# Second FFN of a hybrid diffusion step: first weights loaded before the output stage, the input's remaining blocks in a set order, inner rows stored whole and split in the down stage

## The chip, the cores and the metric

The kernel runs on one core of a Trainium2 chip. The metric is device time in microseconds (us) of one execution. Before the change three runs gave 3045.46, 3050.65 and 3051.04 us, median 3050.65. Engines: PE (TensorE matmuls; PEld is its weight load), DVE (VectorE), ACT (ScalarE), POOL (GpSimd), SP (SyncE, which here only issues DMAs).

## The reference

The reference is two layers of a backbone, 1024 latent and 128 context tokens, model width 1024. Each layer is a mixer and a gated conv FFN with sandwich norms. The change touches the FFN of the second layer:

```python
def conv_ffn(h, w_up, cw, cb, w_down):
    u = dwconv(h @ w_up, cw, 1) + cb          # w_up 1024 x 5632, 3 taps over tokens
    g, val = jnp.split(u, 2, axis=-1)
    return (jax.nn.gelu(g) * val) @ w_down    # w_down 2816 x 1024
xs = _post(xs, conv_ffn(_pre(xs, m_s, norm_g[l, 2], 1), *ffw), m_s, norm_g[l, 3], 1)
```

All of it is float32.

## The kernel before

T = 1152 tokens stand in NT = 9 tiles of 128; the FFN's inner 2816 channels in NFB = 22 blocks of 128. A float32 matmul is made of three fast ones: each operand is split into a high part (a copy into the type F32R on ACT) and a low part (a subtraction on DVE or POOL), and hi·hi, hi·lo and lo·hi are added up in PSUM (`pair`, L1519, and `split` functions).

**The output stage before the FFN** (`mixer_out`, L1390): for each token tile, a 1024x1024 product, the norm and residual, the next norm, a transpose, and `Blocks.put`, which writes the FFN's input.

**The FFN's input as blocks** (`Blocks`, L57). The up product uses a scheme with 7 products in place of 8: the input is cut into quarters 11, 12, 21, 22 (channels by tokens, half each) and weights likewise; each block of 128 channels and its gate partner needs the products of `PRODS` (L1560): S2·T2, S1·T1, w11·11, S4·22, w12·21, S3·T3, w22·T4. S1 to S4 are sums of weight quarters, T1 to T4 of input quarters. `put` makes T1 and T2 and splits them as the tiles come. `rest` (L91) splits 11, 22, 21 and builds and splits T3 and T4: for each of six items four chunks of 128x576.

**The up stage** (`up`, L1526): for block n `load` brings the weights of value and gate (512 KB each) on SP's queue; `split(n, i)` makes the weight sums on POOL and the split of product i, on POOL for i = 0 and 3, on DVE otherwise; `prod` runs 24 matmuls of 128x288; `evict` adds the products together; `up_rest` (L1642) is the convolution (rows of three taps, ACT once, DVE four times), the gelu, the product with the value (L1665), the split of that row (copy L1666 on ACT, subtraction L1667 on POOL) and two stores to DRAM (L1669). `order` runs the products of block n with product 6 of block n-1 behind the first of block n. Weights are loaded two blocks ahead, and weight splits have three buffers. `H.rest` stands in the program behind the first product.

**The down stage** (`early` in `layers`, L1970, and `down2`, L1690): three groups of 8, 7 and 7 blocks; for each group and token tile, `down_rows` (L1682) loads hi and lo rows of that tile from DRAM with two DMAs on POOL's queue (three buffers), 48 or 42 matmuls of 128x512 follow, and the sums are copied (first group, ACT) or added (DVE, L1714). `down_w` (L1674) loads one block of w_down on SP's queue and splits it on DVE or POOL. `early` starts the first of both before the up stage's last product is out.

**What sets the order.** The program that builds the kernel orders each engine's instructions itself, from estimated durations: it issues what its estimate has ready, earlier in the program first. Waits are placed by it for every dependence. A new pool of buffers lies over the memory of closed ones, and its buffers wait for what was there. `behind(i, p)` (L183) forces i after p on one engine.

Of the kernel before, what the change touches and what calls it, by code (L numbers as in the profile page):

```python
# [17 lines left out]
T = 1152  # L18
# [38 lines left out]
class Blocks:  # L57
# [12 lines left out]
    def put(self, k, t, q, ps, sc, sh):  # L70
        nc = k.nc
        V, G, A = nc.vector, nc.gpsimd, nc.scalar
        for n in range(2):
            c0, c1 = max(t * 128, n * HT), min(t * 128 + 128, n * HT + HT)
            if c0 < c1:
                for i in range(4):
                    b = q * 4 + i
                    A.activation(self.raw["12"[q] + "12"[n]][:, i, c0 - n * HT:c1 - n * HT], ps[:, i, c0 - t * 128:c1 - t * 128],
                                 AF.Identity, scale=sc[:, b:b + 1], bias=sh[:, b:b + 1])
        if t * 128 + 128 > HT and q:  # L80
            cs = slice(max(t * 128 - HT, 0), t * 128 + 128 - HT)
            R = lambda x: self.raw[x][:, :, cs]
            t1, t2 = (k.cv.tile([128, 4, 128], F32, tag="cv", name=k.nm("t"))[:, :, :cs.stop - cs.start] for _ in range(2))
            V.tensor_tensor(t1, R("12"), R("11"), op=OP.subtract)
            V.tensor_tensor(t2, R("22"), t1, op=OP.subtract)
            for x, s, e in (("T2", t2, V), ("T1", t1, G)):
                h, l = self.hi[x][:, :, cs], self.lo[x][:, :, cs]
                A.activation(h, s, AF.Copy)
                e.tensor_tensor(l, s, f(h), op=OP.subtract)

    def rest(self, k):  # L91

        nc = k.nc
        V, G, A = nc.vector, nc.gpsimd, nc.scalar
        new = lambda n, tag=None: (k.big if tag else k.big2).tile([128, 4, HT], F32R, tag=tag or "big2", name=k.nm(n))

        def split(x, src, e):
            for i in range(4):
                A.activation(self.hi[x][:, i], src[i], AF.Copy)
                e.tensor_tensor(self.lo[x][:, i], src[i], f(self.hi[x][:, i]), op=OP.subtract)  # L100
        raw = {x: [r[:, i] for i in range(4)] for x, r in self.raw.items()}
        temp = lambda: [t[:, i] for t in [k.mid.tile([128, 2, HT], F32, tag="cc", bufs=4, name=k.nm("tf")) for _ in range(2)] for i in range(2)]
        self.hi["11"], self.lo["11"] = new("h11"), new("l11")
        split("11", raw["11"], V)
        t3 = temp()
        for i in range(4):
            G.tensor_tensor(t3[i], raw["22"][i], raw["12"][i], op=OP.subtract)
        self.hi["22"], self.lo["22"] = new("h22"), new("l22", "r12")
        split("22", raw["22"], V)
        t4 = temp()  # L110
        for i in range(4):
            V.tensor_tensor(t4[i], raw["21"][i], f(self.hi["T2"][:, i]), op=OP.subtract)
        self.hi["21"], self.lo["21"] = new("h21", "r22"), new("l21", "r11")
        split("21", raw["21"], G)
        self.hi["T3"], self.lo["T3"] = new("T3h"), new("T3l")
        split("T3", t3, V)
        for i in range(4):
            V.tensor_tensor(t4[i], t4[i], f(self.lo["T2"][:, i]), op=OP.subtract)
        self.hi["T4"], self.lo["T4"] = new("T4h"), new("T4l")
        split("T4", t4, V)  # L120
# [27 lines left out]
class K:  # L148
# [1377 lines left out]
    def up(self, l, H, early):  # L1526
# [6 lines left out]
        wt = lambda tag, bufs: self.wr.tile([128, 8, 128], F32, tag=tag, bufs=bufs, name=self.nm("w" + tag))  # L1533
# [5 lines left out]

        def load(n):  # L1540
            u = fbs[n]
            u.g, u.v = wt("g", 2), wt("v", 2)
            for r, b in ((u.v, NFB + n), (u.g, n)):
                nc.sync.dma_start(r, w_up[:, b * 128:b * 128 + 128].rearrange("(k p) c -> p k c", p=128))

        def sums(n, part):
            u = fbs[n]
            if part == 0:
                u.s = wt("s", 1)
                u.w = {"11": u.g[:, 0:4], "12": u.g[:, 4:8], "21": u.v[:, 0:4], "22": u.v[:, 4:8], "S1": u.s[:, 0:4], "S2": u.s[:, 4:8]}  # L1550
                w = u.w
                tt(G, w["S1"], w["21"], w["22"], OP.add)
                tt(G, w["S2"], w["S1"], w["11"], OP.subtract)
            else:
                w = u.w
                tt(G, w["12"], w["12"], w["S2"], OP.subtract)
                tt(G, w["21"], w["11"], w["21"], OP.subtract)
# [4 lines left out]
        def split(n, i):  # L1562

            u = fbs[n]
            if i == 0:
                u.s = wt("s", 1)
# [3 lines left out]
            u.p[i] = self.pair(u.w[PRODS[i][0]], PRODS[i][2], self.wr, "p", 3)  # L1570
            if i == 1:
                w = u.w
                w["S4"], w["S3"] = w["S2"], w["21"]
                tt(G, w["S4"], w["12"], w["S2"], OP.subtract)
                tt(G, w["S3"], w["11"], w["21"], OP.subtract)
# [42 lines left out]
        load(0)  # L1618
        load(1)
        split(0, 0)  # L1620
        split(0, 1)
        rests = []
        for m, (n, i) in enumerate(order):
# [3 lines left out]
            if m == 0:  # L1627
                H.rest(self)
# [13 lines left out]
    def up_rest(self, l, fb, C):  # L1642
# [39 lines left out]
    def down_rows(self, l, gi, t):  # L1682
        m = self.scratch(f"m{l}", [2, NFB, 128, T])
# [213 lines left out]
    def layers(self, late, fctx, rctx):  # L1897

        nc, a = self.nc, self.a
        with ExitStack() as ctx:  # L1900
            P = lambda name, bufs, **kw: ctx.enter_context(self.P(name, bufs, **kw))
            self.wr, self.cv, self.w, self.C1 = P("wr", 2), P("cv", 4), P("w", 4), P("C1", 1)
# [63 lines left out]
        self.wr, self.mid, self.big2 = P("wru", 1), P("midu", 1), P("big2", 7)  # L1966
# [12 lines left out]
        self.up(1, H, early)  # L1979
# [34 lines left out]
```

## Time and profile before

| | |
|---|---|
| median of three runs | 3050.65 us |
| profiled execution | 3047.32 us, span 3045.5 us, mean PE clock 0.964 |
| busy: PE | 2785.9 us, 91% |
| PEld | 2509.3 us, 82% |
| DVE | 2123.9 us, 70% |
| ACT | 1148.2 us, 38% |
| POOL | 1227.1 us, 40% |
| DMA | 331.46 MB, mean 109 GB/s |

The profile is that of one execution. Busy shares are means over the whole span, and matmul ends are modelled. Where the FFN in question lies: the output stage ends near 2174 us, up products run from 2214.66 to 2747, down matmuls from 2753 to 3036.

### The profile page before, as it was taken

To read this page: it belongs to the slowest core of one execution; us is meant where nothing else is said; L and a number is where in the kernel's file an instruction comes from. 1 tells how busy PE (TensorE), PEld (TensorE's weight loads), DVE (VectorE), ACT (ScalarE), POOL (GpSimd) and SP (SyncE) were. 2 spreads that over 40 slices of the span, in tenths; PEclk is the share of its full clock that TensorE was granted. 3 is DMA by queue.
4 is the path that set the end of the run, shared out by engine and by line. 5 is a ranking of instruction groups with operands and counts; after the bars stand their busy time and mean duration, and the time that the engine had idled before them with its cause. 6 is when DMAs were issued, how large, how long until landed. Compare 5 with 4: busy or idle time off the path is not lost.

```text
span 3045.5 us, 42039 instructions
## 1 busy us (share of the span) xinstructions
PE 2785.9 (91%) x15724; PEld 2509.3 (82%) x15724; DVE 2123.9 (70%) x3330; ACT 1148.2 (38%) x1946; POOL 1227.1 (40%) x1218
## 2 busy tenths in 40 slices
PE   7977788988899999999999989999589999998998
PEld 3875566777789999999999879997489999996887
DVE  6777766997468888888555765555678888884113
ACT  5222113766353222222222465564543444443101
POOL 2699972876131000000000341111467777765312
PEclk9988899999899999999999989999899999999999
DMA  6434447543543333333111221124213222229766
GB/s 219 140 87 113 116 132 210 137 103 103 162 149 96 92 97 89 95 93 93 46 43 51 97 94 52 59 98 141 90 62 100 89 89 89 89 83 251 138 109 157
DMA packets 357738, 331.46 MB, mean 109 GB/s; under 512 B 47134, under 2 KB 312050, under 8 KB 357534
## 3 DMA queue, kind: packets, MB, share of 16 engines
q1 hardware_dynamic: 273656, 264.47, 27.9%
q0 software_dynamic: 66464, 49.16, 9.0%
q10 hardware_dynamic: 17414, 15.14, 1.8%
q8 instruction: 124, 2.03, 0.3%
q14 instruction: 80, 0.66, 0.1%
HBM read 246.54 MB, written 82.16 MB: 108 GB/s over the span
## 4 chain that ended last, share of the span: by engine, by line
PE 46%; POOL 8%; DVE 8%; issue 6%; DMA 1%; ACT 1%; ACTq 0%; POOLq 0%; DVEq 0%; SPq 0%
PE pps L181 25%; PE dps L181 8%; PE dps L1706 8%; PE ops L181 3%; DVE cc L1659 3%; POOL C L1532 3%; POOL ws L1532 2%; POOL wv L1532 1%; DVE wp L1523 1%; DMA mt<-m 1%; POOL wp L1523 1%; PE gps L181 1%; DVE C L1532 1%; POOL hl L54 1%; PE sps L1585 0%
## 5 line engine op out<-in xcount | busy, mean ns | idle before, releaser
L181 PE MATMUL pps<-hh,whi 128*128 128x384 f32 (+1 forms) x1824 | 625.9, 344 | 0.4 <-ACT qr L1020 0.4
L181 PE MATMUL pps<-hl,whi 128*128 128x384 f32 (+1 forms) x1824 | 624.9, 343 | 1.4 <-DVE hl L878 0.8
L181 PE MATMUL pps<-hh,wlo 128*128 128x384 f32 (+1 forms) x1824 | 623.6, 342 | 2.3 <-DVE wlo L193 2.3
L181 PEld LDWEIGHTS pps<-hh,whi 128*128 128x128 f32 x1824 | 347.5, 191 | 11.6 <-issue 3.2
L181 PEld LDWEIGHTS pps<-hh,wlo 128*128 128x128 f32 x1824 | 347.2, 190 | 8.7 <-DVE wlo L193 3.2
L193 POOL TENSOR_TENSOR wlo<-wr,whi 128x1024 fp32r<-128x1024 f32 x22 | 56.5, 2580 | 739.3 <-PE dps L181 596.2
L181 PEld LDWEIGHTS pps<-hl,whi 128*128 128x128 f32 x1824 | 347.5, 191 | 7.2 <-DVE hl L878 1.6
L1706 PE MATMUL dps<-wp,mt 128*128 128x512 f32 x1188 | 278.7, 396 | 10.7 <-DMA mt<-m 10.7
L1706 PEld LDWEIGHTS dps<-wp,mt 128*128 128x128 f32 x1188 | 224.3, 189 | 64.9 <-ACT wp L1522 6.4
L1659 DVE SCALAR_TENSOR_TENSOR cc<-C,cvc,cc 128x1023 f32<-128x1023 f32 (+1 forms) x176 | 244.0, 1425 | 39.9 <-ACT cc L1654 39.9
L1453 DVE SCALAR_TENSOR_TENSOR cc<-pps,cvc,cc 128x384 f32<-128x384 f32 (+2 forms) x352 | 171.0, 509 | 39.1 <-ACT cc L1450 37.2
L1585 PE MATMUL sps<-h,wp 128*128 128x288 f32 x1056 | 188.8, 297 | 4.5 <-DVE wp L1523 4.5
L318 DVE SCALAR_TENSOR_TENSOR macc<-mw,sil,macc 128x256 f32<-128x256 f32 x392 | 176.1, 485 | 18.7 <-DMA mw<-w_mod 17.7
L1499 DVE TENSOR_TENSOR acc<-acc,dps 128x512 f32<-128x512 f32 x180 | 122.3, 680 | 77.8 <-PE dps L181 77.2
L191 ACT ACTIVATE whi<-wr 128x1024 fp32r<-128x1024 f32 x102 | 107.6, 1057 | 156.9 <-PE pps L181 101.7
L1184 POOL TENSOR_TENSOR wl<-wf,wh 128x512 fp32r<-128x512 f32 (+2 forms) x96 | 144.8, 1526 | 50.0 <-DVE ra L1154 40.7
L1585 PEld LDWEIGHTS sps<-h,wp 128*128 128x128 f32 x1056 | 155.9, 188 | 9.0 <-DVE wp L1523 9.0
L181 PE MATMUL dps<-whi,mh 128*128 128x512 f32 x396 | 156.4, 395 | 1.2 <-DVE acc L1499 1.2
L181 PE MATMUL dps<-wlo,mh 128*128 128x512 f32 x396 | 156.2, 394 | 0.0
L181 PE MATMUL dps<-whi,ml 128*128 128x512 f32 x396 | 154.9, 391 | 0.0
L1450 ACT ACTIVATE cc<-pps,cvc 128x385 f32<-128x385 f32 (+1 forms) x132 | 87.4, 665 | 177.1 <-PE pps L181 161.5
L193 DVE TENSOR_TENSOR wlo<-wr,whi 128x1024 fp32r<-128x1024 f32 x80 | 100.4, 1256 | 53.0 <-PE pps L181 35.1
(428 smaller groups left out, 6416.4 us busy)
## 6 DMA issues: line engine op xcount, KB each, us to landing
mw<-w_mod SPq DMA_DIRECT2D x224, 128.0 KB
m<-cc SPq DMA_DIRECT2D x44, 576.0 KB
x<-x SPq DMA_DIRECT2D x45, 512.0 KB
wr<-ffn_w_up SPq DMA_DIRECT2D x44, 512.0 KB
wr<-ffn_w_down SPq DMA_DIRECT2D x44, 512.0 KB
wm<-w_mod SPq DMA_DIRECT2D x40, 512.0 KB
mt<-m POOLq DMA_DIRECT2D x36, 448.0 KB, 5.2
k<-kh POOLq DMA_DIRECT2D x8, 1408.0 KB, 6.4
```

The costliest lines, as they stand in the source:

```text
L181: nc.tensor.matmul(ps, x, y, start=first and i == 0 and j == 0, stop=last and i == n - 1 and j == 2)
L191: nc.scalar.activation(hi, raw, AF.Copy)
L193: (eng or nc.vector).tensor_tensor(lo, raw, f(hi), op=OP.subtract)
L318: nc.vector.scalar_tensor_tensor(acc[v], wt, s, acc[v], op0=OP.mult, op1=OP.add)
L1184: pin((nc.vector if late else nc.gpsimd).tensor_tensor(vl, u.wf[b][:, :k], f(vh), op=OP.subtract))
L1450: nc.scalar.activation(cc[:, :no], ps[:, q:q + no], AF.Identity, bias=cw[3], scale=cw[1])
L1453: nc.vector.scalar_tensor_tensor(cc[:, oa - o0:ob - o0], ps[:, oa + d - i0:ob + d - i0], cw[j], cc[:, oa - o0:ob - o0], op0=OP.mult, op1=O ...
L1499: nc.vector.tensor_tensor(acc[t][:, sl], acc[t][:, sl], ps, op=OP.add)
L1532: tt = lambda e, o, x, y, op: e.tensor_tensor(o, x, y, op=op)
L1585: nc.tensor.matmul(ps[:, c, :W2], w, z[:, c * W2:c * W2 + W2], start=m == 0, stop=m == len(steps) - 1)
L1659: nc.vector.scalar_tensor_tensor(cc[:, o0:o1], src[:, o0 + d:o1 + d], cw[j], cc[:, o0:o1], op0=OP.mult, op1=OP.add)
L1706: nc.tensor.matmul(ps[:, h], mt[:, x, i], W[fb][:, y, h * 512:h * 512 + 512], start=i == 0 and j == 0, stop=i == n - 1 and j == 2)
```

## The change

Three edits. (1) `up_first` issues the loads of block 0's weights ahead of `mixer_out`, into two buffers of the pool that held weights there and that now stays; blocks with an even number use these two, odd ones two buffers of the new pool. Block 0's first two splits get a priority 600 places earlier. (2) `rest` keeps each of its instructions behind the one before it on its engine, the first behind `put`'s last splits and, on POOL, behind block 0's last weight sum; block 21's split goes from POOL to DVE, T3's from DVE to POOL, and block 21's comes before T4 is begun. (3) `up_rest` stores the inner row unsplit, in one DMA, the last block's on POOL's queue; `down_rows` loads the unsplit row on SP's queue into a pool that it shares with the raw w_down blocks (six buffers, was four), and `down2` splits it (ACT and DVE) into two buffers, was three.

```diff
@@ Blocks.put, Blocks.rest
-                A.activation(h, s, AF.Copy)
-                e.tensor_tensor(l, s, f(h), op=OP.subtract)
+                self.last = [A.activation(h, s, AF.Copy), e.tensor_tensor(l, s, f(h), op=OP.subtract)] + (self.last if x == "T1" else [])
-    def rest(self, k):
+    def rest(self, k, last):
+        first = self.last + [last]
+        def after(i):
+            for p in [p for p in first if p.ins.engine == i.ins.engine]:
+                k.behind(i, p)
+                first.remove(p)
+            first.append(i)
...
         split("22", raw["22"], V)
+        self.hi["21"], self.lo["21"] = new("h21", "r22"), new("l21", "r11")
+        split("21", raw["21"], V)
         t4 = temp()
         for i in range(4):
-            V.tensor_tensor(t4[i], raw["21"][i], f(self.hi["T2"][:, i]), op=OP.subtract)
-        self.hi["21"], self.lo["21"] = new("h21", "r22"), new("l21", "r11")
-        split("21", raw["21"], G)
+            after(V.tensor_tensor(t4[i], raw["21"][i], f(self.hi["T2"][:, i]), op=OP.subtract))
         self.hi["T3"], self.lo["T3"] = new("T3h"), new("T3l")
-        split("T3", t3, V)
+        split("T3", t3, G)
@@ up
+    def up_first(self, l):
+        out = []
+        for b in (NFB, 0):
+            out.append(self.wr.tile([128, 8, 128], F32, tag="wr", name=self.nm("w0")))
+            self.nc.sync.dma_start(out[-1], self.a["ffn_w_up"][l][:, b * 128:b * 128 + 128].rearrange("(k p) c -> p k c", p=128))
+        return out
...
+        fbs[0].v, fbs[0].g = first
-            u.g, u.v = wt("g", 2), wt("v", 2)
+            u.v, u.g = (self.wr.tile([128, 8, 128], F32, tag="wr", name=self.nm("w" + x)) if n % 2 == 0 else wt(x, "gv", 2) for x in "vg")
...
-        load(0)
         load(1)
-        split(0, 0)
-        split(0, 1)
+        with self.tc.high_priority(offset=600):
+            split(0, 0)
+            split(0, 1)
...
-                H.rest(self)
+                H.rest(self, fbs[0].last)
@@ up_rest
-        nc.scalar.activation(h.bitcast(F32R), m, AF.Copy)
-        nc.gpsimd.tensor_tensor(m, m, h, op=OP.subtract)
-        for x, y in enumerate((h, m)):
-            nc.sync.dma_start(self.scratch(f"m{l}", [2, NFB, 128, T])[x, fb], y)
+        (nc.gpsimd if fb == NFB - 1 else nc.sync).dma_start(self.scratch(f"m{l}", [NFB, 128, T])[fb], m)
@@ down_rows, down2
-        mt = self.dm.tile([128, 2, len(fbs), 128], F32R, tag="dm", name=self.nm("mt"))
-        for x in range(2):
-            self.nc.gpsimd.dma_start(mt[:, x], m[x, fbs[0]:fbs[-1] + 1, :, t * 128:t * 128 + 128].rearrange("f p t -> p f t"))
-        return mt
+        r = self.wrd.tile([128, len(fbs), 128], F32, tag="wr", name=self.nm("mr"))
+        self.nc.sync.dma_start(r, self.scratch(f"m{l}", [NFB, 128, T])[fbs[0]:fbs[-1] + 1, :, t * 128:t * 128 + 128].rearrange("f p t -> p f t"))
+        return r
-                mts = [rows.pop((gi, t)) if (gi, t) in rows else self.down_rows(l, gi, t) for t in ts]
+                mts = [self.pair(rows.pop((gi, t)) if (gi, t) in rows else self.down_rows(l, gi, t), nc.vector, self.dm, "dm") for t in ts]
@@ layers
+        self.wr = fctx.enter_context(self.P("wr", 2))
...
+            first = self.up_first(1)
             self.mixer_out(1, W, lambda t: x2[t * 128:t * 128 + 128], x3, H, keep)
...
-            self.wrd, self.wd0, self.dm = R("wrd", 4), R("wd0", 4), R("dm", 3)
+            self.wrd, self.wd0, self.dm = R("wrd", 6), R("wd0", 4), R("dm", 2)
```

In the stretch of `rest` not shown every instruction is wrapped in `after(...)`.

## Rows read from the trace of the kernel before

**Rows 1.** Stretches: PE, PEld, DVE, ACT, POOL busy (instructions), PEclk, DMA share, GB/s.
```profile
2173.74:2214.66 40.92, 3.23 (x18) 2.50 (x17) 35.46 (x33) 22.01 (x46) 24.05 (x17) 0.58 0.22 64
2478.89:2503.21 24.32, 22.86 (x169) 22.39 (x169) 21.20 (x20) 9.98 (x13) 17.75 (x9) 1.00 0.28 92
2747.03:2800.40 53.37, 42.65 (x171) 33.52 (x172) 28.19 (x16) 19.87 (x19) 31.01 (x15) 0.90 1.22 287
2800.40:3036.20 235.80, 235.80 (x1018) 190.81 (x1017) 48.91 (x52) 22.57 (x29) 56.94 (x62) 1.00 0.76 137
```

**Rows 2.** Timeline of PE: start, duration, line, tile, [idle before <-releaser].
```profile
2173.74 0.40 PE L181 MATMUL ops<-Wo,yl 128*128 128x512 f32 x1
...
2214.66 0.85 PE L1585 MATMUL sps<-T2h,wp 128*128 128x288 f32 x2 [31.20 <-ACT wp L1522]
...
2239.28 0.43 PE L1585 MATMUL sps<-T4h,wp 128*128 128x288 f32 x2
```

**Rows 3.** Timelines of ACT, DVE, POOL, SP's queue, 2182 to 2216 us.
```profile
2182.64 2.90 ACT L78 ACTIVATE b<-tps,mc,mc 128x128 f32<-128x128 f32 x8 [2.86 <-PE tps L369]
...
2185.57 1.10 DVE L85 TENSOR_TENSOR t<-b,t 128x512 f32<-128x512 f32 x1 [0.70 <-ACT b L78]
2186.60 10.14 DVE L100 TENSOR_TENSOR l<-b,h 128x576 fp32r<-128x576 f32 x8
...
2203.55 7.15 DVE L100 TENSOR_TENSOR T3l<-tf,T3h 128x576 fp32r<-128x576 f32 x4
...
2213.30 2.75 DVE L100 TENSOR_TENSOR T4l<-tf,T4h 128x576 fp32r<-128x576 f32 x4
...
2197.53 7.35 POOL L100 TENSOR_TENSOR l<-b,h 128x576 fp32r<-128x576 f32 x4 [4.09 <-ACT h L99]
2204.84 1.77 POOL L1532 TENSOR_TENSOR ws<-wv 128x512 f32<-128x512 f32 x1
...
2182.54 0.57 SPq L1544 DMA_DIRECT2D wg<-ffn_w_up  x1
```

**Rows 4.** Timelines in the loop, and what PE waited for on L1585.
```profile
2472.70 1.82 POOL L1532 TENSOR_TENSOR C<-U,X 128x576 f32<-128x576 f32 x1 [2.76 <-DVE U L1532]
2474.47 2.69 POOL L1667 TENSOR_TENSOR cc<-cc,cc 128x1152 f32<-128x1152 f32 x1
2477.10 1.73 POOL L1523 TENSOR_TENSOR wp<-ws,wp 128x512 fp32r<-128x512 f32 x1
...
2473.12 0.61 ACT L1522 ACTIVATE wp<-ws 128x512 fp32r<-128x512 f32 x1
...
2475.89 1.83 DVE L1523 TENSOR_TENSOR wp<-wv,wp 128x512 fp32r<-128x512 f32 x1
2477.64 3.58 DVE L1659 SCALAR_TENSOR_TENSOR cc<-C,cvc,cc 128x1023 f32<-128x1023 f32 x2
...
2235.27 1.54 DVE L1659 SCALAR_TENSOR_TENSOR cc<-C,cvc,cc 128x1023 f32<-128x1023 f32 x2 [0.82 <-ACT cc L1654]
...
2478.89 0.80 PE L1585 MATMUL sps<-T2h,wp 128*128 128x288 f32 x4 [1.23 <-POOL wp L1523]
...
  POOL wp L1523: 24.5, 21
  DVE wp L1523: 4.5, 19
```

**Rows 5.** PE's first down matmul; DMA queues (packets, MB, share) 2700-2860, 2180-2215 us.
```profile
2753.22 1.19 PE L1706 MATMUL dps<-wp,mt 128*128 128x512 f32 x2 [6.18 <-DMA mt<-m]
...
q0 software_dynamic: 22368, 11.27, 51.8%
...
q1 hardware_dynamic: 4160, 2.10, 21.7%
```

**Rows 6.** DVE in the down stage: ns min/median/max, first and last start.
```profile
L1523 DVE TENSOR_TENSOR wp<-wr,wp x11: 1219/2533/3586, 2747.4 to 2862.1; 128x1024 fp32r<-128x1024 f32 x11
...
L1714 DVE TENSOR_TENSOR acc<-acc,dps x18: 1220/1222/1223, 2870.8 to 3036.5; 128x1024 f32<-128x1024 f32 x18
```

More of the change, by code (lines that the diff above doesn't have):

```diff
@@ L95, in rest @@
         new = lambda n, tag=None: (k.big if tag else k.big2).tile([128, 4, HT], F32R, tag=tag or "big2", name=k.nm(n))
+        first = self.last + [last]
[4 more added lines that the diff above has]
+            first.append(i)
         def split(x, src, e):
             for i in range(4):
-                A.activation(self.hi[x][:, i], src[i], AF.Copy)
-                e.tensor_tensor(self.lo[x][:, i], src[i], f(self.hi[x][:, i]), op=OP.subtract)
+                after(A.activation(self.hi[x][:, i], src[i], AF.Copy))
+                after(e.tensor_tensor(self.lo[x][:, i], src[i], f(self.hi[x][:, i]), op=OP.subtract))
         raw = {x: [r[:, i] for i in range(4)] for x, r in self.raw.items()}
@@ L106, in rest @@
         for i in range(4):
-            G.tensor_tensor(t3[i], raw["22"][i], raw["12"][i], op=OP.subtract)
+            after(G.tensor_tensor(t3[i], raw["22"][i], raw["12"][i], op=OP.subtract))
         self.hi["22"], self.lo["22"] = new("h22"), new("l22", "r12")
         split("22", raw["22"], V)
+        self.hi["21"], self.lo["21"] = new("h21", "r22"), new("l21", "r11")
+        split("21", raw["21"], V)
         t4 = temp()
         for i in range(4):
-            V.tensor_tensor(t4[i], raw["21"][i], f(self.hi["T2"][:, i]), op=OP.subtract)
-        self.hi["21"], self.lo["21"] = new("h21", "r22"), new("l21", "r11")
-        split("21", raw["21"], G)
+            after(V.tensor_tensor(t4[i], raw["21"][i], f(self.hi["T2"][:, i]), op=OP.subtract))
         self.hi["T3"], self.lo["T3"] = new("T3h"), new("T3l")
-        split("T3", t3, V)
+        split("T3", t3, G)
         for i in range(4):
-            V.tensor_tensor(t4[i], t4[i], f(self.lo["T2"][:, i]), op=OP.subtract)
+            after(V.tensor_tensor(t4[i], t4[i], f(self.lo["T2"][:, i]), op=OP.subtract))
         self.hi["T4"], self.lo["T4"] = new("T4h"), new("T4l")
@@ L1524, in pair, with up @@
         return p
-    def up(self, l, H, early):
+    def up_first(self, l):
[4 more added lines that the diff above has]
+        return out
+    def up(self, l, H, first, early):
         nc = self.nc
@@ L1532, in up @@
         tt = lambda e, o, x, y, op: e.tensor_tensor(o, x, y, op=op)
-        wt = lambda tag, bufs: self.wr.tile([128, 8, 128], F32, tag=tag, bufs=bufs, name=self.nm("w" + tag))
+        wt = lambda n, tag, bufs: self.wu.tile([128, 8, 128], F32, tag=tag, bufs=bufs, name=self.nm("w" + n))
         W2 = HT // 2
@@ L1538, in up @@
         fbs = [Fb() for _ in range(NFB)]
+        fbs[0].v, fbs[0].g = first
         def load(n):
             u = fbs[n]
-            u.g, u.v = wt("g", 2), wt("v", 2)
+            u.v, u.g = (self.wr.tile([128, 8, 128], F32, tag="wr", name=self.nm("w" + x)) if n % 2 == 0 else wt(x, "gv", 2) for x in "vg")
             for r, b in ((u.v, NFB + n), (u.g, n)):
                 nc.sync.dma_start(r, w_up[:, b * 128:b * 128 + 128].rearrange("(k p) c -> p k c", p=128))
[L1546 to L1557, printed above, removed]
         PRODS = (("S2", "T2", G), ("S1", "T1", V), ("11", "11", V), ("S4", "22", G), ("12", "21", V), ("S3", "T3", V), ("22", "T4", V))
@@ L1565, in split @@
             if i == 0:
-                u.s = wt("s", 1)
+                u.s = wt("s", "s", 1)
                 w = u.w = {"11": u.g[:, 0:4], "12": u.g[:, 4:8], "21": u.v[:, 0:4], "22": u.v[:, 4:8], "S1": u.s[:, 0:4], "S2": u.s[:, 4:8]}
@@ L1569, in split @@
                 tt(G, w["S2"], w["S1"], w["11"], OP.subtract)
-            u.p[i] = self.pair(u.w[PRODS[i][0]], PRODS[i][2], self.wr, "p", 3)
+            u.p[i] = self.pair(u.w[PRODS[i][0]], PRODS[i][2], self.wu, "p", 3)
             if i == 1:
@@ L1574, in split @@
                 tt(G, w["S4"], w["12"], w["S2"], OP.subtract)
-                tt(G, w["S3"], w["11"], w["21"], OP.subtract)
+                u.last = tt(G, w["S3"], w["11"], w["21"], OP.subtract)
         def prod(n, i):
@@ L1978, in early @@
                     rows[0, i] = self.down_rows(1, 0, i)
-        self.up(1, H, early)
+        self.up(1, H, first, early)
         return rows
```

5 lines of the change are left out of this document (2 added, 3 removed).

## The prediction

> **What bounds the kernel now.** I read the page's slices first: TensorE is busy in nearly all of the span and its granted clock is high, so time can come only from stretches where it waits. Then the stretches around the edited code. Four differ [rows 1]. Between the last output matmul and the first FFN product PE works 3.23 of 40.92 us at a mean clock of 0.58. In the product loop a feature block takes 24.32 us, of which PE works 22.86 and DVE 21.20. From the end of the products to the start of the even down stage PE works 42.65 of 53.37 us. After that it works 235.80 of 235.80: the down stage has nothing to give, and can only lose. The order in time [rows 2]: output ends at 2173.74, the first product starts at 2214.66 after 31.20 us of waiting, and block 0's last product (T4, the eighth in the order) starts at 2239.28.
>
> **Part A: first weights early, rest in a set order.** In the old order the first weights are issued at 2182.54 and their first sum S1 runs on POOL at 2204.84, behind four splits of block 21 that took 7.35 us [rows 3]. So the first product waited for nearly all of H.rest. With the weights loaded before the output stage and both splits put ahead, what is left before the first product is T2 itself. Token tile 8's last half leaves ACT at 2182.64+2.90 = 2185.5, the second difference takes 1.10 (2186.7), its two split steps some 0.65 each as the ACT split of that size took 0.61 [rows 4] (2188.0). S1, S2 and the first splits now run on POOL and ACT just then, where the norm's small steps also stand; I add 1 us: first product at 2189, not 2214.66.
>
> That is 25.7 us earlier, but not 25.7 us gained, since H.rest now runs beside the products and they need it. It has 24 DVE instructions, which in the old trace took from 2186.60 to 2213.30+2.75 = 2216.05, 29.4 us [rows 3]. The new list has 24 again: block 21's split goes from POOL to DVE, T3's from DVE to POOL. On POOL there were 8 and there are 8. The DVE group beside POOL work took 7.15/4 = 1.8 us each (T3l), the group without it 2.75/4 = 0.69 (T4l), so the pace is set by the company, which stays alike: rest again ends some 29 us after its start, near 2218. Then what can PE do meanwhile? A product is 24 matmuls; at (24.32-1.46)/168 = 0.136 us each (1.46 is PE's idle share of a period) it takes 3.27 us, the first ones about 2 us more at the low clock. Products 0 and 1 need T2, T1; product 2 needs the 11 split, the first four DVE instructions at 1.8 (ready at +7, PE there at +8): no stall. Product 3's weight split is on POOL behind T3's and t3's eight instructions of 1.8 = 14.4 and its own 1.7 (+17; PE there at +12). Product 4's weight split is on DVE, and stands later in the program than rest: I take it behind rest, +30. Products 4, 5 and the next block's first follow at 3.27 each, so T4's starts at 2189+30+9.8 = 2229 against 2239.28: 10 us. From that I take 1 for the output stage, into whose first tiles 1 MB of weights now falls. **A = 9 us.** Bounds: without any stall T4 starts at 2189+7x3.27+4 = 2216, 23 us; if all from product 2 on wait for rest's end it starts at 2218+5x3.27 = 2234.5, and with 2 us of late loads 3 us are left.
>
> **Part B: rows stored whole.** Each block loses an ACT copy, the POOL subtraction (2.69 us) and one of two stores. Follow one period [rows 4]: POOL finishes C at 2472.70+1.82 = 2474.5, does the row's subtraction to 2477.16, and only then the next block's first weight split (1.73), whose hi part ACT had ready at 2473.7. PE waits 1.23 us for that split, though it reached the place at 2477.66. Without the subtraction the split runs at 2474.5 to 2476.2, 1.4 us before PE asks. Over the loop PE waited 24.5 us for POOL's splits and 4.5 for DVE's: 29.0 in all. What is late next is DVE: 21.20 busy of 24.32, in a chain with few gaps, so taking away PE's wait alone would not shorten it. But DVE's own instructions there are stretched: its split beside the subtraction takes 1.83, and the two taps behind it 3.58, where the same two took 1.54 beside no POOL work. POOL's work now ends some 2.6 us earlier, so most of the taps' 2.0 us comes back. DVE's round would then be 24.32-2.0 = 22.3, under PE's 22.86, and PE binds. I leave PE 0.2 us of waiting a period for DVE, 4 us in 21 periods: **B = 29-4 = 25 us.** Bounds: 31 (every wait and restart gone, 21x1.46), and 8 where DVE's chain gives back only 0.4 a period.
>
> A rule weighs here. The trace shows DVE's split (started 2475.89) ending just 0.56 us after POOL's subtraction ends at 2477.16 [rows 4]. The Trainium skill, "SBUF — State Buffer", section "Who interferes with whom", says that a DVE instruction with two SBUF inputs and a GpSimd instruction that reads SBUF exclude each other for whole instructions. By it the 2.69 us could come back to DVE entire; DVE would be at 21.6, and B at its upper bound.
>
> **Part C: rows loaded whole, split in the down stage.** From the end of the products to 2800.40 PE ran 171 matmuls, which at 235.80/1018 = 0.2316 take 39.6 of the 53.4 us: 13.8 are lost, 6.18 of them in one wait for the first row [rows 1, 5]. The software queue moved 22368 packets in 51.8% of 16 engines over 160 us, 59 ns a packet; the same 512-byte packets of the first FFN weights on SP's queue took 21.7% over 35 us for 4160, 29 ns. A row tile of 1024 packets on SP then costs 1.9 us of all engines, where two took 7.6. So rows and W_down land sooner. Against it, each row's split needs ACT and DVE, and DVE at that time still has the last block's taps; a split of 1024 elements took 1.22 to 3.59 on DVE, 2.53 in the median [rows 6]. SP's queue also now carries rows behind W_down loads that wait for six shared buffers. I set 3 us of gain between -4 (first rows' split behind all of the last taps) and +9. **C = 3 us.** Afterwards 27 row splits of 2.5 us are 68 us on DVE, which was busy 48.91 of 235.80 [rows 1], and they hide there: a row tile lasts PE 9.7 to 11.1 us (42 or 48 matmuls). If that cover went, see the third rival. The last row's store on POOL's queue, the four up-weight buffers split over two pools, and the kernel's tail cost nothing: the last row is first read in the third group, and the tail has none of it.
>
> **Sum.** 9+25+3 = 37 us off the profiled execution's 3047.3 gives 3010. That execution lies 3.3 under the runs' median, 1.9 over the lowest; I say 3011.
>
> **Rivals.** One: DVE keeps the loop. Its chain still has waits that POOL's subtraction does not cause (for ACT's row start, for C), and with rest behind, it starts the loop in arrears. B is then 8, A and C as above: 3047-20 = 3027. For it: DVE's 87%; against it: the taps' stretch.
>
> Two: everything comes back. The order lets product 4's split run between rest's instructions, A is 18, B 31 and C 6: 3047-55 = 2992. For it: PE, not DVE, would be the longest engine in the loop. The Trainium skill's rule above would give B's share of this rival and says nothing of the other two.
>
> Three, the other side: the split of row t+1 comes on DVE behind the addition of tile t's sums (1.22, 18 of them [rows 6]), which waits for PE's last matmul of t. Then PE waits at each of the tiles for addition and split, 1.22+1.22 and a fraction for two hand-overs, 2.7 us; at 24 tiles 65 us. It decides as soon as a wait of over 1.5 us a tile shows up (37/24). 3047+65-37 = 3075. For it: only two split buffers instead of three, and program order. Against it: the old trace shows S1 behind block 21's splits, which stand later in the program [rows 3], so order follows readiness, and the split is ready while PE still works on tile t.
>
> Four: the change does not do what it says at the start, the first products stay behind rest (A = 0), the new DVE splits cost C its 4, and B is 8: 3043, no measurable change.
>
> **How the numbers follow.** Forecast 0.46 (3002 to 3020), rival one 0.18, two 0.19, three 0.10, four 0.07. Left out by 2988 to 3036: three, four and a little of two, 0.2. Changes of 0.2% (6 us) are about what can be told here; faster 0.83, same 0.06, slower 0.11.
>
> **What would show it.** A: first product within 20 us of the last output matmul, T4's start before 2232, PE idle before products 3 and 4. B: a period of 22.9 to 23.2 us, no POOL wait before T2's product, taps of 1.5 us for two. C: first down matmul within 6 us of the last product; in the even stage PE still without a gap. Wrong would be a period over 24, a first product after 2200, or DVE named before down matmuls more than a few times.

## The result and the profile after

The changed kernel takes 3001.51 us (median of four runs, 2997.61 to 3005.14), the kernel before, beside it on the same chip, 3050.38: a ratio of 0.9843 [0.9824, 0.9862], 49 us less. A second comparison on another chip gave 0.9844 [0.9831, 0.9857]. The forecast was 3011 in a range of 2988 to 3036; the measured median lies just under the band that the prediction gave its forecast (3002 to 3020), towards rival two (2992).

The traced execution of the changed kernel took 3004.82 us, that of before 3047.32. Its last output matmul, up to which the code differs only in the two weight loads issued earlier, starts 3.9 us later (2177.68, before 2173.74 [rows 2]). In the fourteen traces of this study that matmul starts anywhere from 2170.55 to 2182.01, and the two kernels without the early loads (2173.74 and 2178.10) lie inside that, so the 1 us that the prediction took off for the loads can't be seen. I measure from that matmul, stretch by stretch. The changed kernel's stretches, which answer to [rows 1] (columns as there: from the last output matmul to the first product; one period of the loop; the end of the products and the start of the down stage; the even down stage):

```profile
2177.68:2196.04 18.36, 3.24 (x18) 2.51 (x16) 12.19 (x13) 14.77 (x34) 8.58 (x9) 0.66 0.26 86
2452.62:2474.95 22.33, 22.33 (x170) 22.33 (x169) 19.19 (x20) 9.26 (x12) 14.58 (x9) 1.00 0.23 74
2706.36:2759.73 53.37, 45.36 (x181) 36.09 (x181) 30.30 (x20) 21.20 (x21) 21.70 (x9) 0.90 0.68 209
2759.73:2993.76 234.03, 234.00 (x1010) 189.18 (x1008) 69.66 (x74) 43.22 (x51) 16.46 (x20) 1.00 0.29 90
```

In the second row PE is busy 22.33 of 22.33 us: the loop has become PE's. The first row shows the stretch ahead of the first product cut from 40.92 to 18.36 us. The loss between products and down stage went from 10.7 to 8.0 us of idle PE.

PE's timeline at the start, the rows with a wait and two of T4's (start, duration, tile, [idle before <-releaser]), answering to [rows 2]:

```profile
2177.68 0.40 PE L189 MATMUL ops<-Wo,yl 128*128 128x512 f32 x1
...
2196.04 0.85 PE L1590 MATMUL sps<-T2h,wp 128*128 128x288 f32 x2 [8.64 <-ACT wp L1530]
2200.89 1.33 PE L1590 MATMUL sps<-T1h,wp 128*128 128x288 f32 x4 [1.60 <-DVE wp L1531]
2215.30 0.53 PE L1590 MATMUL sps<-h,wp 128*128 128x288 f32 x2 [1.64 <-ACT wp L1530]
...
2226.54 1.33 PE L1590 MATMUL sps<-h,wp 128*128 128x288 f32 x4 [9.38 <-DVE wp L1531]
2237.20 0.43 PE L1590 MATMUL sps<-T4h,wp 128*128 128x288 f32 x2
2237.74 0.69 PE L1590 MATMUL sps<-T4h,wp 128*128 128x288 f32 x4
```

The three terms, each from one trace of either kernel:

| stretch | before | after | measured | forecast |
|---|---|---|---|---|
| A: last output matmul to T4's first product | 65.54 | 59.52 | 6.0 | 9 |
| B: T4's first product to the last product's end | 507.75 | 469.16 | 38.6 | 25 |
| C: last product's end to the last addition's end | 290.67 | 288.62 | 2.0 | 3 |

Together 46.7 against the forecast 37; the later start of the traced execution takes 3.9 back.

### The profile page after: what moved, and what is told of

The parts are those of the page before. It is cut to its first block, busy times and chain, and to the rows that moved or that the text cites. A ratio compares the mean times of both kernels' runs of the same rounds, so it can differ in the third digit from the quotient of the medians.

```text
span 3003.0 us, 41912 instructions
## 1 busy us (share of the span) xinstructions
PE 2785.0 (93%) x15724; PEld 2514.4 (84%) x15724; DVE 2109.8 (70%) x3357; ACT 1155.1 (38%) x1951; POOL 1101.3 (37%) x1143
## 4 chain that ended last, share of the span: by engine, by line
PE 62%; DVE 3%; issue 3%; POOL 1%; ACT 1%; DMA 1%; ACTq 0%; POOLq 0%; DVEq 0%; SPq 0%
PE pps L189 26%; PE sps L1590 16%; PE dps L189 8%; PE dps L1707 8%; PE ops L189 3%; PE gps L189 1%; POOL hl L54 0%; DMA mw<-w_mod 0%; DVE l L108 0%; PE tps L377 0%; DVE yl L1423 0%; POOL tf L115 0%; POOL rs L239 0%; PE mps L334 0%; DVE macc L326 0%
## 5 line engine op out<-in xcount | busy, mean ns | idle before, releaser
L201 POOL TENSOR_TENSOR wlo<-wr,whi 128x1024 fp32r<-128x1024 f32 x22 | 54.6, 2490 | 741.2 <-PE dps L189 595.7
L1707 PE MATMUL dps<-wp,wp 128*128 128x512 f32 x1188 | 279.4, 397 | 8.0 <-DVE C L1548 5.9
L1707 PEld LDWEIGHTS dps<-wp,wp 128*128 128x128 f32 x1188 | 225.3, 190 | 61.9 <-ACT cc L1667 6.1
L1664 DVE SCALAR_TENSOR_TENSOR cc<-C,cvc,cc 128x1023 f32<-128x1023 f32 (+1 forms) x176 | 225.6, 1321 | 35.6 <-ACT cc L1659 35.6
L1548 POOL TENSOR_TENSOR C<-U,X 128x576 f32<-128x576 f32 x44 | 105.4, 2395 | 135.5 <-DVE U L1548 135.5
```

Of the source, the lines that this page charges most:

```text
L201: (eng or nc.vector).tensor_tensor(lo, raw, f(hi), op=OP.subtract)
L1548: tt = lambda e, o, x, y, op: e.tensor_tensor(o, x, y, op=op)
L1664: nc.vector.scalar_tensor_tensor(cc[:, o0:o1], src[:, o0 + d:o1 + d], cw[j], cc[:, o0:o1], op0=OP.mult, op1=OP.add)
L1707: nc.tensor.matmul(ps[:, h], mt[:, x, i], W[fb][:, y, h * 512:h * 512 + 512], start=i == 0 and j == 0, stop=i == n - 1 and j == 2)
```

## The experiments

"The stretch of the products" is that of term B, "the last product" the end of the products counted from the last output matmul (573.3 us before, 528.7 and 529.1 in two traces of the changed kernel).

**Each part alone.** Start only: the old store and the old rows are put back in the changed kernel.

```diff
-        (nc.gpsimd if fb == NFB - 1 else nc.sync).dma_start(self.scratch(f"m{l}", [NFB, 128, T])[fb], m)
+        nc.scalar.activation(h.bitcast(F32R), m, AF.Copy)
+        nc.gpsimd.tensor_tensor(m, m, h, op=OP.subtract)
+        for x, y in enumerate((h, m)):
+            nc.sync.dma_start(self.scratch(f"m{l}", [2, NFB, 128, T])[x, fb], y)
...
```

> The kernel before with the early first weights and the set order of the rest alone; rows are still split and stored as two halves. My theory (the parts add): the start is that of the changed kernel, first product 18 us after the output stage's last matmul and T4's first product 59.5 us after it (65.5 before), so 6 us come back; the loop keeps its period of 24.3 us with PE's waits for GpSimd in it, and the stretch from T4's first product to the products' end stays near 507 us. Whole: about 6 us under the kernel before, within 2 us. Rival (the set order of the rest also cures the loop, since buffers and instruction order changed with it): that stretch falls under 490 us and the whole by 20 us or more.

Rows only: the same lines the other way round in the kernel before.

> The kernel before with the rows stored whole and split in the down stage alone; weights and rest start as before. My theory: first product again 41 us after the output stage's last matmul and T4's first product 65.5 us after it; the loop's period falls from 24.3 to 22.2 us, T4's first product to the products' end takes 469 us where it took 507.6, and the down stage loses 2 us. Whole: about 40 us under the kernel before. Rival (the loop was freed by the start's new buffers and order): the stretch stays over 495 us and the whole is less than 15 us under before.

Start only took 3044.69 us, a ratio of 0.9985 [0.9975, 0.9995]; rows only 3008.95, 0.9877 [0.9854, 0.9901]. T4's first product came 59.85 and 65.55 us after the last output matmul. The stretch of the products in the start-only and then in the rows-only kernel (columns as above):

```profile
2241.86:2750.42 508.56, 479.37 (x3530) 469.96 (x3528) 440.31 (x401) 211.97 (x274) 366.21 (x191) 1.00 0.28 92
```

```profile
2243.65:2712.81 469.16, 469.16 (x3530) 468.92 (x3528) 398.68 (x400) 198.06 (x255) 295.49 (x164) 1.00 0.23 76
```

The parts add: counted from the last output matmul the last product ends 4.9 us earlier with the start alone, 38.6 with the rows alone, and 44.6 with both; by run medians, on different chips, 3.8 and 39.5 stand against 47.8 to 48.9. The rows alone free the loop. 469.16 us is to the hundredth what the changed kernel takes: the same 3530 matmuls without a gap.

**The subtraction put back, unused.** The row is still stored whole; ACT's copy and POOL's subtraction run again behind it.

```diff
         (nc.gpsimd if fb == NFB - 1 else nc.sync).dma_start(self.scratch(f"m{l}", [NFB, 128, T])[fb], m)
+        nc.scalar.activation(h.bitcast(F32R), m, AF.Copy)
+        nc.gpsimd.tensor_tensor(h, m, h, op=OP.subtract)
```

> The changed kernel with work added that nothing reads: behind each inner row ScalarE's rounded copy and GpSimd's subtraction of the row run again as they did before; the row is still stored whole, once, and split in the down stage. My theory (GpSimd's 2.7 us subtraction ahead of the next block's weight sums made PE wait, the stores and their halves did not): the period goes back to 24.0 to 24.4 us, PE's waits for GpSimd ahead of the first product of a block are there again, T4's first product to the products' end takes 500 to 508 us, and the whole is 32 to 40 us slower than the changed kernel. Rival (the second store, the doubled bytes, or the row's buffer held longer made PE wait): the period stays at 22.2 to 22.5 us and the whole within 6 us of the changed kernel.

It took 3048.28 us, a ratio to the kernel before of 0.9997 [0.9988, 1.0006]; the stretch of the products took 508.60. Some 46 us over the changed kernel (timed on other chips) are more than the 32 to 40 I expected: the loop's 39.4 are as expected, but the added work also stands ahead of the first down matmuls, and the last stretch took 293.1 in place of 288.6. One period on POOL, DVE and PE, and PE's waits from 2240 to 2690 us (total, times, longest):

```profile
2401.15 2.68 POOL L1673 TENSOR_TENSOR cc<-cc,cc 128x1152 f32<-128x1152 f32 x1
2403.78 1.72 POOL L1531 TENSOR_TENSOR wp<-ws,wp 128x512 fp32r<-128x512 f32 x1
...
2402.56 1.82 DVE L1531 TENSOR_TENSOR wp<-wv,wp 128x512 fp32r<-128x512 f32 x1
2404.30 3.58 DVE L1664 SCALAR_TENSOR_TENSOR cc<-C,cvc,cc 128x1023 f32<-128x1023 f32 x2
...
2405.55 0.80 PE L1590 MATMUL sps<-T2h,wp 128*128 128x288 f32 x4 [1.22 <-POOL wp L1531]
...
PE sps L1590 <- POOL wp L1531: 20.8, 17, 1.2
PE sps L1590 <- DVE wp L1531: 5.8, 19, 1.4
```

These are the rows of before [rows 4] to within 0.02 us: subtraction, late split, PE's 1.22, and the two taps at 3.58. The same place in the changed kernel:

```profile
2452.62 1.80 POOL L1548 TENSOR_TENSOR C<-U,X 128x576 f32<-128x576 f32 x1 [2.77 <-DVE U L1548]
2454.39 1.29 POOL L1531 TENSOR_TENSOR wp<-ws,wp 128x512 fp32r<-128x512 f32 x1
2455.76 1.30 POOL L1548 TENSOR_TENSOR ws<-wg,ws 128x512 f32<-128x512 f32 x1
...
2455.79 1.81 DVE L1531 TENSOR_TENSOR wp<-wv,wp 128x512 fp32r<-128x512 f32 x1
2457.53 1.53 DVE L1664 SCALAR_TENSOR_TENSOR cc<-C,cvc,cc 128x1023 f32<-128x1023 f32 x2
```

The split follows C (a tile in which `evict` adds up products, as U is) at once, the taps take 1.53, and PE has no wait. That the row was stored twice, or its bytes, had no part in the loop's time. ACT's copy came back together with the subtraction, and no run parts the two; PE's waits name POOL's split and not ACT's.

**The subtraction in POOL's idle time.** The same two operations, but POOL's is held behind the next block's S4.

```diff
+                if self.sub and order[m + 2][1] == 1:
+                    h, r = self.sub.pop(0)
+                    self.behind(tt(G, h, r, h, OP.subtract), fbs[order[m + 2][0]].s4)
```

> The same added copy and subtraction, read by nothing, but GpSimd's subtraction is ordered behind the next block's weight sums, where GpSimd has an idle stretch of some 9 us in each period. Theory one (the subtraction's place in GpSimd's order cost the time): the period is 22.2 to 22.6 us and the whole within 7 us of the changed kernel. Theory two (GpSimd and VectorE slow one another wherever the subtraction stands, VectorE's share being the tight one): the period is 23 us or more, VectorE's 128x2x288 taps or splits are longer than in the changed kernel (1.53 and 1.81 us), and the whole is 15 us or more slower.

It took 3071.63 us, slower than the kernel before (1.0075 [1.0060, 1.0090]), with 538.7 in the products. My premise was wrong. In the changed kernel POOL is idle 22.33-14.58 = 7.75 us a period, but in pieces of 2.75, 2.01 and 2.77 us, each a wait for another engine's result; the subtraction (2.69 us by itself) would just fill the longest. In the place that it got, less was free. POOL around the moved subtraction, and DVE's split beside it:

```profile
2464.65 1.29 POOL L1548 TENSOR_TENSOR ws<-wg,ws 128x512 f32<-128x512 f32 x1
2465.89 3.12 POOL L1548 TENSOR_TENSOR cc<-cc,cc 128x1152 f32<-128x1152 f32 x1
2468.99 1.88 POOL L1548 TENSOR_TENSOR C<-U,X 128x576 f32<-128x576 f32 x1
...
2467.07 2.50 DVE L1531 TENSOR_TENSOR wp<-ws,wp 128x512 fp32r<-128x512 f32 x1
```

C can't start until 2468.99 though DVE's U was there at 2467.15, 1.3 us after the subtraction began; ACT's and DVE's taps wait for C, and the next weight split on DVE stands behind the taps. From 2300 to 2490 us the period is 24.0 with one wait of PE for DVE of 1.4; later the planned order differs, PE's clock falls to 0.86 of full in places and more is lost, which I have not followed up. The two theories are not told apart by it: the place delays C, and the split beside the subtraction takes 2.50 us where one without POOL work beside it takes 0.68.

**What won the start.** First weights asked for behind the output stage in the program, and then the rest without its set order:

```diff
-            first = self.up_first(1)
             self.mixer_out(1, W, lambda t: x2[t * 128:t * 128 + 128], x3, H, keep)
+            first = self.up_first(1)
```

> The changed kernel with block 0's first two weight tiles asked for behind the output stage's code in place of ahead of it; all else as changed. Theory one (the start was won by the set order of the rest; the weights landed in time before too): first product 18 to 20 us after the output stage's last matmul, T4's first product within 2 us of 59.5 us after it, whole within 2 us of the changed kernel. Theory two (the early load won it): the first product waits for the weights, 30 us or more after the output stage's last matmul, T4's first product 64 us or more after it, whole 4 to 8 us slower than the changed kernel.

```diff
-            for p in [p for p in first if p.ins.engine == i.ins.engine]:
+            for p in []:
...
-            first.append(i)
+            pass
```

> The changed kernel without the set order: the same instructions of the rest, left to the planner. Theory one (the set order won the start): first product near 41 us after the output stage's last matmul again and T4's first product 64 to 67 us after it, whole 4 to 8 us slower than the changed kernel. Theory two (the early weights and the raised priority of the first two splits suffice): first product 15 to 20 us and T4's first product 55 to 60 us after it, whole within 2 us of the changed kernel.

The late place changed nothing (3004.53 us; T4's first product at 59.41): the two loads still went out at 2021.99 and 2078.56, as in the changed kernel at 2019.8 and 2075.8, since the builder issues what its buffers allow. So this run doesn't show what late weights would cost. Without the set order the kernel took 3011.29, and PE's first product:

```profile
2214.86 0.85 PE L1590 MATMUL sps<-T2h,wp 128*128 128x288 f32 x2 [28.53 <-ACT wp L1530]
```

That is 38.27 us after the last output matmul, and the last product ended 537.4 us after it, later even than in the rows-only kernel (534.7). With the weights there 100 us before, the first products still stand behind the rest. The set order is what won the start: without it, the other edits to the start left T4's first product 68.24 us after the last output matmul, 2.7 later than before. Whether the order would win as much with weights loaded as late as before, no run shows.

**The start, further.** The changed kernel's wait of 9.38 us for product 4's split suggested three edits: the rest's eight POOL operations on DVE; the rest in two parts, with product 4's split between them; and both, in three parts, each held behind the split that the next products need. In the last two the rest's first POOL operation, where it has one, also stands behind S4 in place of S3.

```diff
-            after(G.tensor_tensor(t3[i], raw["22"][i], raw["12"][i], op=OP.subtract))
+            after(V.tensor_tensor(t3[i], raw["22"][i], raw["12"][i], op=OP.subtract))
...
-        split("T3", t3, G)
+        split("T3", t3, V)
```

> The changed kernel with the rest's eight GpSimd operations (four subtractions for T3, four for its low part) on VectorE, order as before. Theory one (VectorE is slowed by GpSimd beside it, its 128x576 operations take 1.8 us there and 0.74 us alone): VectorE's operations of the rest fall to 0.74 to 0.9 us each, so that its 24 of them take about 20 us where its 20 took about 30; T4's first product comes 47 to 52 us after the output stage's last matmul (59.5 in the changed kernel), whole 7 to 12 us faster than the changed kernel. Theory two (VectorE's durations are its own, and eight more operations lengthen its queue): T4's first product 60 us or more after it, whole the same or up to 8 us slower.

```diff
+        yield
         t4 = temp()
...
         split("T4", t4, V)
+        yield
...
-                H.rest(self, fbs[0].last)
+                rest = H.rest(self, fbs[0].last)
+            if m in (0, 2):
+                next(rest)
```

> The changed kernel with the rest in two parts: T4's and T3's building is put behind the third product, so that product 4's weight split stands ahead of it on VectorE, and the rest's first GpSimd operation follows S4 in place of S3, so that product 0's low part is not behind the four subtractions for T3. Theory one (the wait of 9.4 us for product 4's split is order alone): the wait goes, T4's first product comes 51 to 56 us after the output stage's last matmul, whole 4 to 8 us faster than the changed kernel. Theory two (VectorE's total work up to T4 is the bound of the start): the wait moves to T4's own product, which comes 58 to 60 us after it, and the whole stays within 2 us.

Neither helped: 3002.40 and 3000.38 us, T4's first product at 56.35 and 60.23, the last product at 528.4 and 529.8. The first of these T4 times lies between what the two theories gave (52 at the most, 60 at the least). With the rest on VectorE, sharing showed from both sides. (I had miscounted: 32 operations of the rest stand on DVE then, 24 in the changed kernel.) The 32 took 31.6 us where the 24 took 33.9. But POOL, DVE and PE of that kernel:

```profile
2214.49 7.93 POOL L1531 TENSOR_TENSOR wp<-ws,wp 128x512 fp32r<-128x512 f32 x1 [11.89 <-ACT wp L1530]
...
2212.60 2.75 DVE L122 TENSOR_TENSOR tf<-b,T2h 128x576 f32<-128x576 f32 x4
2215.27 2.76 DVE L108 TENSOR_TENSOR T3l<-tf,T3h 128x576 fp32r<-128x576 f32 x4
2217.95 2.75 DVE L126 TENSOR_TENSOR tf<-tf,T2l 128x576 f32<-128x576 f32 x4
...
2222.48 1.33 PE L1590 MATMUL sps<-h,wp 128*128 128x288 f32 x4 [5.63 <-POOL wp L1531]
```

POOL's split, 1.29 us by itself, took 7.93 while DVE ran without a pause, and PE waited 5.63 for it. In two parts, the wait for product 4's split went, but another took its place ahead of block 1's first product, with ACT's T4 copies named as what came last, much as the second theory had it:

```profile
2223.72 0.82 PE L1592 MATMUL sps<-T2h,wp 128*128 128x288 f32 x2 [5.74 <-ACT T4h L107]
```

> The changed kernel itself, beside the next three on the same chip, to set them against. Every theory: some 47 us under the kernel before, T4's first product 59.5 us after the output stage's last matmul.

```diff
+        first += yield
         self.hi["21"], self.lo["21"] = new("h21", "r22"), new("l21", "r11")
...
+        first += yield
         t4 = temp()
...
-                H.rest(self, fbs[0].last)
+                rest = H.rest(self, fbs[0].last)
+            if m < 3:
+                rest.send(list(self.pairs) if m else None)
```

> The changed kernel with the rest wholly on ScalarE and VectorE and in three parts, each behind the weight split that the next products need: blocks 11 and 22 and T3's subtraction, then block 21 behind product 3's split, then T3 and T4 behind product 4's split. Theory one (both the sharing with GpSimd and the order cost the start its time, and taking one away alone showed the other): the last product ends 517 to 523 us after the output stage's last matmul (528.3 in the changed kernel), whole 5 to 11 us faster than the changed kernel. Theory two (a GpSimd split of 1.3 us can't start while VectorE works without a pause, as when it took 7.9 us in the kernel with the rest on VectorE): product 3's low part, still on GpSimd, again comes 6 us or more late, the last product ends 526 us or more after it, whole within 3 us of the changed kernel.

```diff
-            u.p[i] = self.pair(u.w[PRODS[i][0]], PRODS[i][2], self.wu, "p", 3)
+            u.p[i] = self.pair(u.w[PRODS[i][0]], PRODS[i][2] if n else V, self.wu, "p", 3)
```

> The same in three parts, and block 0's two weight splits that stood on GpSimd (products 0 and 3) are on VectorE as well; GpSimd is left the weight sums. Theory one (order and sharing): last product 516 to 522 us after the output stage's last matmul, whole 6 to 12 us faster than the changed kernel. Theory two (a GpSimd operation starves beside a busy VectorE): here alone the gain shows, 5 us or more over the kernel that keeps the two splits on GpSimd. Theory three (VectorE's queue is the bound of the start whatever stands on it): last product 526 us or more after it, whole within 3 us of the changed kernel.

The changed kernel again took 3002.33 us, the rest in three parts 2997.74, without POOL's splits 3000.40. The last product came at 529.1, 526.0 and 526.7 us: 3.1 and 2.4 us gained, half of what I had expected at the least. Theory one failed for both. Of the second kernel's theories, theory two (a GpSimd operation starves; 5 us or more over the first) failed too, and theory three, that VectorE's queue bounds the start whatever stands on it, met both its numbers (526 or more, within 3 us of the changed kernel). In the first, product 3's split on POOL was not late (1.34 us), against theory two. The changed kernel again and the rest in three parts, 50 us from the first product on:

```profile
2194.44:2244.44 50.00, 37.56 (x232) 36.51 (x233) 44.65 (x39) 19.70 (x29) 36.35 (x23) 0.78 0.07 22
```

```profile
2194.88:2244.88 50.00, 41.30 (x268) 39.63 (x268) 45.95 (x49) 20.48 (x32) 27.56 (x15) 0.91 0.07 22
```

In three parts PE is 36 matmuls ahead by then, 4.8 us at 22.33/168 = 0.133 each; 1.3 of that goes in two waits for DVE's splits behind it (0.34 and 0.92), which stand behind the rest's last operations and evictions. DVE works 45 to 46 of the 50 us in both. The four runs of each overlap, 2993.8 to 3003.6 against 2999.3 to 3006.1, so the gain is seen in the traces only.

**The rows' queue.** Rows loaded through POOL's queue as before, but whole:

```diff
-        self.nc.sync.dma_start(r, self.scratch(f"m{l}", [NFB, 128, T])[fbs[0]:fbs[-1] + 1, :, t * 128:t * 128 + 128].rearrange("f p t -> p f t"))
+        self.nc.gpsimd.dma_start(r, self.scratch(f"m{l}", [NFB, 128, T])[fbs[0]:fbs[-1] + 1, :, t * 128:t * 128 + 128].rearrange("f p t -> p f t"))
```

> The changed kernel with the down stage's rows read back through GpSimd's queue as before, whole and split in the down stage as changed. Theory one (the 2 us of the down stage came with the queue: its packets took 52% of the queue's time before and 38% on SP's): the stretch from the last product to the last addition is 289 to 291 us (287.4 in the changed kernel), whole 1 to 4 us slower. Theory two (half as many bytes, whichever queue): the stretch stays at 286.5 to 288 us and the whole within 1.5 us.

It took 3001.92 us, and the last stretch 286.6, less than in the changed kernel, as theory two had it: the queue won nothing. What PE waited for in the down stage, before and then after:

```profile
PE dps L1706 <- DMA mt<-m: 10.7, 4, 6.2
```

```profile
PE dps L1707 <- DVE C L1548: 5.9, 1, 5.9
PE dps L1707 <- ACT wp L1530: 1.6, 1, 1.6
PE dps L1707 <- DVE wp L1531: 0.5, 1, 0.5
```

All waits named after rows are gone, and 2.7 of 10.7 us with them. But the start-only kernel, which stores and loads its rows in two halves as before, has the same 8.0 us in all, in a stretch of 288.14:

```profile
PE dps L1711 <- DVE C L1548: 5.9, 1, 5.9
PE dps L1711 <- DMA mt<-m: 2.1, 3, 0.9
```

Its first wait is for the last block's own additions (tile C), and is as long with old rows as with new. Behind it stand 2.1 us of waits for rows; the changed kernel has 2.1 us of waits for splits in their place. Between kernels with the same down stage the stretch differs (285.9 with the rest in two parts, 288.8 in the changed kernel again), with PE's mean clock of its first 40 us at 0.91 and 0.87. At 0.91 it is 288.1 with old rows (start only) and 287.7 with new (rows only), at 0.87 290.7 and 288.6 (the two traces of the table). A term C of 2 us is inside that.

## Why the prediction was right, and where it was not

That it is faster, the order of the three terms and the mechanism of B held. The sum was 10 us too small: B was 13.6 too small, and A and C, 4 too large together, hid part of it.

**B was mis-sized: 38.6 for 25, above its bound of 31.** The step that was mis-sized is "DVE's round would then be ... under PE's 22.86, and PE binds". 22.86 is PE's busy time in a period that has two waits, and I took it for the floor. The floor is 22.33. Per period 24.32-22.33 = 2.0 us came back, while the waits in it were 1.46. The rest hangs on each wait: PE's busy time counts the last matmul ahead of it to its modelled end, and four matmuls behind it take 0.80 (the row with the wait of 1.22 above) where four in a running row take 0.69. Two in a running row take 0.43 and four 0.69, so one matmul is recorded as 0.30 against a step of 0.13. That makes 0.17+0.11 = 0.28 us a wait. Of the 40 waits [rows 4] 39 lie in B's stretch, 28.4 us; with 39x0.28 = 10.9 that makes an estimate of 39.3, near the 38.6 measured. The Trainium skill, "Perfetto Trace Analysis", section "Tensor Engine Instruction (MATMUL, LD_WEIGHTS)", says that a matmul's end is computed and not observed; the rows agree, since consecutive matmuls recorded as 0.30 long start 0.13 apart. The 4 us that I left for DVE's waits were also not needed: no wait of PE was left in the loop. DVE's busy time fell from 21.20 [rows 1] to 19.19 a period, as forecast, and rival one, DVE keeping the loop, is refuted. Rival two's condition for B, PE as the longest engine of the loop, came true.

**The rule on sharing.** The Trainium skill, "SBUF — State Buffer", section "Who interferes with whom", has a DVE instruction with two SBUF inputs contend with a GpSimd instruction that reads SBUF. By it the prediction let DVE get back all of 2.69 us, with B at its upper bound. DVE got back 2.0 of busy time a period, and B went beyond the bound for the reason above, not by this rule. The exclusion itself shows in the traces: of the 104 weight splits on DVE in B's stretch 41 took over 1 us before and 20 in the changed kernel, each of them ending 0.55 to 0.56 us after a POOL instruction ended; the others took 0.7. The split in [rows 4] gained nothing (1.83 before, 1.81 now): it stands beside POOL's next weight sum in place of the subtraction. The two taps fell from 3.58 to 1.53 with POOL idle beside them, and with the subtraction put back they took 3.58 again. The POOL split of 7.93 us is the other side of it: it lasted through a run of DVE instructions and not just one.

**A: 6.0 for 9.** The set order did what it should, and PE got past product 4's split 30.5 us after the first product, where I said 30. That this number fits is luck. I had the split behind all of the rest, which was to end 29 us after its start. The rest's DVE instructions took 33.9 us, not 29, and the last ended 42.9 us after the first began, but the split ran between them (2225.81, below). Rival two had that order, and gave A 18 for it. The miss is ahead of it: "first product at 2189", 15 us after the last output matmul, was 18.36. POOL and DVE of the changed kernel:

```profile
2190.09 1.27 POOL L88 TENSOR_TENSOR T1l<-t,T1h 128x512 fp32r<-128x512 f32 x1 [5.26 <-ACT T1h L88]
2191.31 1.72 POOL L1548 TENSOR_TENSOR ws<-w 128x512 f32<-128x512 f32 x1
2193.11 1.67 POOL L1548 TENSOR_TENSOR ws<-ws,w 128x512 f32<-128x512 f32 x1
...
2196.49 7.43 POOL L115 TENSOR_TENSOR tf<-b,b 128x576 f32<-128x576 f32 x4
2203.88 1.29 POOL L1531 TENSOR_TENSOR wp<-ws,wp 128x512 fp32r<-128x512 f32 x1
2207.68 1.70 POOL L1531 TENSOR_TENSOR wp<-ws,wp 128x512 fp32r<-128x512 f32 x1 [0.74 <-ACT wp L1530]
...
2191.83 7.20 DVE L108 TENSOR_TENSOR l<-b,h 128x576 fp32r<-128x576 f32 x4
...
2225.81 0.68 DVE L1531 TENSOR_TENSOR wp<-w,wp 128x512 fp32r<-128x512 f32 x1
...
2233.98 0.75 DVE L108 TENSOR_TENSOR T4l<-tf,T4h 128x576 fp32r<-128x576 f32 x1
```

I priced S1 and S2 as running beside the norm's small steps. They stand behind the last T1l on POOL, and S2's high part is what PE waits for. I also had product 3 alone wait for the rest's eight POOL instructions. Its split (2207.68) stands behind four of them, t3's, and so does product 0's own low part (2203.88), so PE began products whose second half it could not do. By itself that cost nothing that showed: with the rest in two parts this split stands ahead of t3, and the last product came no sooner.

**C: 2.0 for 3**, and not resolved: the stretch varies by more between kernels that are the same there. The step that doesn't hold is "6.18 of them in one wait for the first row": the start-only kernel, with old rows, waits 5.91 at that place for tile C, so by that trace faster rows could take little of it. A row's split takes 1.09 us in the even stage (2829.35, say), where I had 2.5. The third rival's order did come about, row splits behind additions on DVE, but for the tile two ahead, so PE never waits: 234.00 busy of 234.03.

The forecast's signs: first product within 20 us (18.36, yes), T4 before 2232 (2237.20, or 2233.3 with the late start taken off: no), PE idle before products 3 and 4 (a little and much), a period of 22.9 to 23.2 (22.33, below), no POOL wait (yes), taps 1.5 (1.53), first down matmul within 6 us (5.89).

## What to carry to other kernels

An engine's floor in a loop is the spacing of its instructions in a run without gaps times their number, not its busy time in a period with waits: each wait costs more than its length. An operation that stands in a queue ahead of the next operand that PE needs can hold up the whole loop: one POOL subtraction, with ACT's copy, cost 2.0 us in each period here. Idle time in pieces is room only if the piece at that place is longer than the operation. Moving the rest's work from POOL to DVE moved the wait too, and gained nothing here; put first in each queue what the next matmul needs.

## What the runs showed of the hardware that I had not expected

A GpSimd subtraction of 128x512 lasted six times its own time (7.93 us for 1.29) beside a VectorE that ran operations of 0.69 us without a pause, and the one for S4 took 4.96 us in the kernel without block 0's GpSimd splits. VectorE's operations beside the first of these are not slowed (2.75 us for four): here the engine that ran without a gap kept the other out. The other way round, VectorE's long splits in the product loop all end 0.55 to 0.56 us after a GpSimd instruction does.

The runs of the kernel before that stood beside the first experiments went from 3044.87 to 3058.53 us, those of the changed kernel from 2997.61 to 3005.14 and from 2999.32 to 3006.08; a change of 2 or 3 us in one stretch shows in traces counted from a common instruction, and not in medians of four runs.
